# A hybrid decoder layer on one core: pinned orders, the rotary swap by transfers, four accumulators, units kept together

## The chip, the core and the metric

One core of a Trainium2 chip runs the kernel. The metric is the device time of one execution in microseconds (us), given as the median of several runs.

## What is computed

One inference step of one decoder layer, for a prompt of 1024 positions and 8 single new positions (T = 1032 columns in all), model width 1024:

```
x = x + RMSNorm(Mixer(RMSNorm(x)));  y = h + RMSNorm(SwiGLU(RMSNorm(h)))
Mixer: one input projection ->
  (a) q, k, v of 3 attention groups (window, dilation) = (128,1), (512,4), (2048,16), 8 heads x 64,
      rotary on q and k, outputs merged by their softmax denominators  -> 512
  (b) Mamba-2 scan: z / xBC / dt, 16 heads x 64, 2 groups, state 128, conv 4, chunks of 128,
      gated RMSNorm -> 1024
  concat (1536) -> one output projection -> 1024
SwiGLU: hidden 2816
def rope(x): x1, x2 = halves of 32;  [x1*cos - x2*sin, x2*cos + x1*sin]
```

Beside the two outputs y it writes the new key/value caches, the convolution rows and the scan states.

## The kernel before, in words

Data lie transposed: 128 partitions of features by T columns. Each float32 factor is split into a high and a low part of a reduced float32 format (`wh`, `wl`; `xh`, `xl`), and a product is taken as hi*hi + lo*hi + hi*lo. The work of TensorE (PE) is cut into **units** (`unit`, L168 to 176): one block of 128 output features by one of three column blocks of 344, eight 128-row slices with three products each, so 24 products into one PSUM bank. `gemm` (L189) loads a weight block (SP queue), casts it on ScalarE (ACT, L163), takes the low part on VectorE (DVE, L164), and runs three units; each unit's result is evacuated by a function that the caller gives.

PSUM has five pools: `psg` (2 banks), `pss` (2), `psa` (2), `pst` (1), `psn` (1). Main units take banks by `gps` (L180), which goes round the list `gpools`; up to the output projection this list is `[psg]`. Side work takes `pss` by `side_ps` (L80), and the attention's tiles `psa`, `pst` and `psn` by `att_ps`.

Order on each engine is set by a planner that goes by numbers of priority, the lower the sooner: `prio(kind)` (L54) hands out a rising number from a start for each kind: evac 1 million, weights 5, side 10, main 50. A PSUM slot is given in the order in which the program's text asks for it. In this frame the text runs:

- input norm, projections for the convolution and dt; the convolution on DVE
- the 16 scan steps `ssd(c, g)` (L479 to 544, eight chunks by two groups) and the decode steps `ssm_decode`, as side work. A scan step: transposes `xt` (PE), `xdt`, `xdd` (DVE), `gb` (PE), `gm` (DVE), eight subtractions `e` (DVE, L516), exp (ACT), e*gm (DVE, L519), `yp` and `yo` (PE), eb*yo (DVE), two operations on GpSimd (POOL), xg+yp and the state `hst` (DVE)
- `pattern(0)`; side `dec_scores(0)`; `pattern(1)`; side `dec_scores(1)`; `pattern(2)`; side `dec_scores(2)`, the merge of the decode outputs and the merge's weights (`wo`, `wtp`, L842). A pattern has four head pairs, each with three projections (v, q, k), the rotary step in `do_qk` and eight attention steps in `attend`. `dec_scores` (L728) transposes rows (`rtp`), sends them to DRAM, reads them back spread over partitions (`qb`), multiplies on POOL, reduces on DVE and transposes the scores (`stp`)
- the z projections (L901), the scan's gated norm, the output projection in two parts (`w_out`, then `att_part` for the attention rows)
- the FFN: for t = 0 and 1 `plain` units (gate `pg`, up `pu`, then silu), for t = 2 to 21 `blocks` that need 7 half-size products of 8, with sums of inputs (`x_sums`) taken ahead; then the output projection (`ffn_out`) and the last norm. Between, `Norms` spreads its two norm parts `first` and `second` over units counted by `GAP` and `step`.

`do_qk` (L610) makes the rotary partner `sw` by four ACT copies of 32 partitions (L615), multiplies by sin on POOL (L616) and by cos on DVE (L617), and adds (L620).

Of the kernel before, what the change touches and what calls it, by code (L numbers as in the profile page):

```python
# [25 lines left out]
LW = 388  # L26
GAP = ((1, 3), (1, 4), (2, 6))
HID = 2816
# [21 lines left out]
def trunk(tc, a, o):  # L50
    nc = tc.nc
    ctr = {"evac": 1_000_000, "w": 5_000_000, "side": 10_000_000, "late": 20_000_000, "main": 50_000_000}

# [113 lines left out]
    def unit(ps, w, hs, ls, c, ch=CH):  # L167
        wh, wl = w  # L168
        c0, c1 = ch[c]
        n = len(hs)  # L170
        with prio("main"):
            for k in range(n):
                ws = slice(k * P, (k + 1) * P)
                for j, (x, y) in enumerate(((wh, hs[k]), (wl, hs[k]), (wh, ls[k]))):
# [7 lines left out]
    def gps(name="g", cw=CW):  # L182
        q = gpools[ngp[0] % len(gpools)]
        ngp[0] += 1
        if q is psg:
            return q.tile([P, 512], F32, tag="g", name=name)[:, :cw]
        return q.tile([P, 512], F32, tag="ap", name=name)[:, :cw]

# [420 lines left out]
    def do_qk(g, hp, which):  # L609
        rw = proj_raw(g * 12 + 4 * which + hp)  # L610
        with prio("side"):
            sw = swpp.tile([P, 3 + T], F32, tag="swp", name="sw")
            for q in range(4):
                s = q ^ 1
                nc.scalar.copy(sw[q * 32:(q + 1) * 32, 0:T], rw[s * 32:(s + 1) * 32, :])  # L615
            nc.gpsimd.tensor_tensor(out=sw[:, 0:T], in0=sw[:, 0:T], in1=sin, op=ALU.mult)  # L616
            nc.vector.tensor_tensor(out=rw, in0=rw, in1=cos, op=ALU.mult)  # L617
            qp = krp if which else qrp
            qr = qp.tile([P, S], F32, tag="qr", name="qr")
            nc.vector.tensor_tensor(out=pview(qr, g), in0=porder(rw, g), in1=porder(sw, g), op=ALU.add)  # L620
            nc.vector.tensor_tensor(out=dec[which][:, g, hp], in0=rw[:, S:T], in1=sw[:, S:T], op=ALU.add)
            if which:
                if g == 1:
                    nc.sync.dma_start(out=o["pk1"][hp].rearrange("p (r i) -> p r i", r=4),
                                      in_=qr.rearrange("p (r i) -> p r i", r=4)[:, :, P:2 * P])
                else:
                    nc.sync.dma_start(out=o[f"pk{g}"][hp], in_=qr[:, S - PKW[g]:S])
        return qr

    def attend(g, hp, qr, kr, vt):  # L630
        nh = nhp.tile([P, S], F32, tag="nh", name="nh")
        for j in range(8):
# [36 lines left out]
            dst = pt[:, 0:2 * nb].rearrange("p q t -> p (q t)")  # L669
            if j % 2 and j % 4 < 2:  # L670
                nc.scalar.copy(dst, tp[:, :2 * nk])
            else:
                nc.vector.tensor_copy(dst, tp[:, :2 * nk])
            if j % 4 == 0:
# [56 lines left out]
    def dec_scores(g):  # L731
# [202 lines left out]
    gst.close()  # L934
    gpools.append(psa)
    ngp[0] = 0
# [52 lines left out]

    def stat(x, first, acc):  # L990
        if first:
            nc.scalar.activation(out=acc, in_=x, func=AF.Square)
# [12 lines left out]
    class Norms:  # L1005
# [12 lines left out]
        def first(self, prev):  # L1018
            c0, c1 = self.c0, self.c1
            with prio("evac"):  # L1020
                r = np_.tile([P, CW], F32, tag="nr", name="nr", bufs=1)
                finish(self.acc, r, prev=prev)
                self.acc = np_.tile([P, CW], F32, tag="nacc", name="nacc2")
                self.h = []
                for i in range(3):
                    n = min(3, KT - 3 * i)
                    x = np_.tile([P, 3, CW], F32, tag="xr", name="xr", bufs=3)
                    nc.sync.dma_start(out=x[:, :n], in_=a["xT"][3 * i:3 * i + n, :, c0:c1].rearrange("k p t -> p k t"))
                    self.h += [x[:, j] for j in range(n)]
                    for m in range(3 * i, 3 * i + n):  # L1030
                        mv, h = mix[m][:, c0:c1], self.h[m]
                        nc.vector.tensor_tensor(out=mv, in0=mv, in1=r, op=ALU.mult)
                        nc.vector.scalar_tensor_tensor(out=h, in0=mv, scalar=nw(MIX_POST, m), in1=h, op0=ALU.mult,  # L1033
                                                       op1=ALU.add)
                        stat(h, m == 0, self.acc)
                    nc.sync.dma_start(out=h_d[3 * i:3 * i + n, :, c0:c1].rearrange("k p t -> p k t"), in_=x[:, :n])

        def second(self, prev):
            c0, c1 = self.c0, self.c1
            with prio("evac"):  # L1040
                r = np_.tile([P, CW], F32, tag="nr", name="nr2", bufs=1)
                finish(self.acc, r, prev=prev)
                for m in range(KT):
                    mv = mix[m][:, c0:c1]
                    nc.vector.scalar_tensor_tensor(out=mv, in0=self.h[m], scalar=nw(FFN_PRE, m), in1=r, op0=ALU.mult,  # L1045
                                                   op1=ALU.mult)
                    nc.scalar.copy(fh[m][:, c0:c1], mv)
                    nc.vector.tensor_tensor(out=fl[m][:, c0:c1], in0=mv, in1=fh[m][:, c0:c1], op=ALU.subtract)  # L1048

# [8 lines left out]
    def att_part(c):  # L1058
        nm = Norms(c)
        for m in range(KT):  # L1060
# [6 lines left out]
            step(last, .5)  # L1067
        ahead.extend([(GAP[c][0], nm.first), (GAP[c][1], nm.second)])

    att_part(0)  # L1070
    att_part(1)
    for m in range(KT):
        step(gemm(a["w_out"][m][:, 512:1536], 1024, sh, sl, ssm_ev(m), cc=(2,), share=True))
    att_part(2)
    right.close()
# [17 lines left out]
    def plain(t, c, w):  # L1093
# [5 lines left out]
        with prio("evac"):  # L1099
            s = np_.tile([P, T], F32, tag="fs", name="fs", bufs=2)[:, :CW]  # L1100
            nc.scalar.activation(out=s, in_=pg, func=AF.Silu)
            next_copy(nc.vector.tensor_tensor(out=s, in0=s, in1=pu, op=ALU.mult))
# [46 lines left out]

    wslots = [(mixp, "mix")] * 8 + [(whp, "wh"), (wlp, "wl"), (whp, "wh"), (wlp, "wl")]  # L1150
    nws = [0]
# [44 lines left out]
    def blocks(t, s, w):  # L1196
# [26 lines left out]
        with prio("evac"):  # L1223
            add(u2, p1, b)
        b = prod("b22")
        with prio("evac"):
            add(v, u2, b)
        b = prod("t3")
        with prio("evac"):
            add(u3, u2, b)  # L1230
        b = prod("t4")
        with prio("evac"):
            next_copy(add(up[:, 0], u3, b))
        b = prod("t1")
        with prio("evac"):
            add(gate[:, 1], v, b)
            add(up[:, 1], u3, b)
            nc.scalar.activation(out=gate, in_=gate, func=AF.Silu)
# [22 lines left out]
    def ffn_out(gi):  # L1261
# [35 lines left out]
        accs = [acct[:, c0:c1] for c0, c1 in CL]  # L1297

        def ev(m, c, ps):
            c0, c1 = CL[c]  # L1300
# [4 lines left out]
            else:  # L1305
                sq = np_.tile([P, T], F32, tag="fs", name="fsq", bufs=2)
                nc.scalar.activation(out=sq[:, :c1 - c0], in_=fv, func=AF.Square)
                nc.vector.tensor_tensor(out=acc, in0=acc, in1=sq[:, :c1 - c0],
                                                                                 op=ALU.add)
            nc.scalar.activation(out=fv, in_=fv, func=AF.Copy, scale=nw(FFN_POST, m))  # L1310
# [8 lines left out]

        def put(c, m, r):  # L1320

            c0, c1 = CL[c]
            fv = fac[m][:, c0:c1]
            nc.vector.tensor_tensor(out=fv, in0=fv, in1=r, op=ALU.mult)
            if c < 2:
# [11 lines left out]
        for c, (c0, c1) in enumerate(CL):  # L1337
            for m in range(KT):
# [133 lines left out]
```

## Time and profile before

| | |
|---|---|
| median of 3 runs | 1892.22 us (1889.53 to 1893.98) |
| profiled execution | 1887.21 us, its span 1885.4 us |
| mean granted clock of PE | 0.975 |
| busy: PE, DVE, ACT, POOL | 1776.3 us (94%), 1151.1 (61%), 781.9 (41%), 323.0 (17%) |
| PE in time: start to 171 us | input norm, convolution and dt projections |
| 171 to 827 us | three attention patterns, the scan, the decode work |
| 827 to 1130 us | z projections, gated norm, output projection |
| 1130 to 1207 us | plain FFN units and the sums for the blocks |
| 1207 to 1603 us, then 1603 to 1885 us | FFN blocks; FFN output, last norm |

Busy time is the time in which an engine executes something; PE's overlapping products count once. The granted clock is 1 at full speed. A wait names the engine and line that waits, and the one that ended the wait.

### The profile page before, as it was taken

The numbers are of one execution on the slowest core, as the hardware profiler recorded it, in microseconds if no ns is written. First come the engines' busy times: TensorE is split into PE (matmuls) and PEld (weight loads), VectorE is DVE, ScalarE is ACT, GpSimd is POOL, SyncE is SP. The second block draws the span as 40 slices with busy tenths as digits, with TensorE's granted clock in tenths as the row PEclk, the third lists the DMA queues.
The fourth block names the chain that finished last, engine by engine and source line by source line (L and its number), as shares of the span: only waits on it lengthen the run. The fifth ranks groups of instructions, "written<-read, shape, count | busy, mean of one in ns | idle before, by whom it ended". The sixth has DMA issues, their size and how long they took to land.

```text
span 1885.4 us, 30770 instructions
## 1 busy us (share of the span) xinstructions
PE 1776.3 (94%) x12207; PEld 1658.5 (88%) x12207; DVE 1151.1 (61%) x2247; ACT 781.9 (41%) x1436; POOL 323.0 (17%) x218
## 2 busy tenths in 40 slices
PE   8999989999998899999789995999999999999995
PEld 6999877888887788988678995899999999999995
DVE  6545667677765544456676699766666665532338
ACT  5533454555554555565242345432232232531133
POOL 0000244544224311133542210000000000000020
PEclk9999999999999999999979998999999999999998
DMA  4322333443325333445755443354544445886686
GB/s 158 133 95 83 104 118 117 139 135 114 99 88 180 114 118 108 148 160 192 190 148 163 128 160 124 118 174 170 171 165 170 172 162 184 314 295 205 214 305 202
DMA packets 135056, 298.61 MB, mean 158 GB/s; under 512 B 18416, under 2 KB 85200, under 8 KB 133504
## 3 DMA queue, kind: packets, MB, share of 16 engines
q1 hardware_dynamic: 134912, 296.64, 47.6%
q8 instruction: 96, 1.57, 0.3%
q14 instruction: 48, 0.39, 0.1%
HBM read 247.49 MB, written 137.10 MB: 204 GB/s over the span
## 4 chain that ended last, share of the span: by engine, by line
PE 38%; DVE 7%; DMA 3%; issue 1%; ACT 1%; POOL 1%; SPq 0%; DVEq 0%; POOLq 0%; ACTq 0%
PE fb L1206 21%; PE g L175 15%; DMA nt<-n_d 2%; PE pg L175 1%; POOL nt L855 1%; DMA hr<-hid_d 1%; DVE xr L1033 1%; PE pu L175 1%; DVE nt L856 1%; DVE nacc L996 1%; DVE sl L925 0%; DVE wl L164 0%; DVE mix L1045 0%; DVE nt L857 0%; DVE fl L1048 0%
## 5 line engine op out<-in xcount | busy, mean ns | idle before, releaser
L175 PE MATMUL g<-xh,wh 128*128 128x344 f32 x1344 | 442.9, 330 | 9.2 <-ACT rw L586 4.9
L175 PE MATMUL g<-xl,wh 128*128 128x344 f32 x1344 | 439.8, 327 | 1.5 <-DVE xl L231 1.5
L175 PE MATMUL g<-xh,wl 128*128 128x344 f32 x1344 | 438.4, 326 | 0.5 <-DVE wl L164 0.5
L175 PEld LDWEIGHTS g<-xh,wh 128*128 128x128 f32 x1344 | 255.3, 190 | 18.9 <-ACT rw L586 7.3
L175 PEld LDWEIGHTS g<-xh,wl 128*128 128x128 f32 x1344 | 255.6, 190 | 12.3 <-issue 11.0
L175 PEld LDWEIGHTS g<-xl,wh 128*128 128x128 f32 x1344 | 255.6, 190 | 10.6 <-issue 7.7
L1206 PE MATMUL fb<-fh,wsl 128*128 128x258 f32 x1280 | 234.6, 283 | 0.9 <-DVE wsl L1176 0.8
L1206 PEld LDWEIGHTS fb<-fh,wsl 128*128 128x128 f32 x1280 | 198.0, 189 | 1.5 <-DVE wsl L1176 0.9
L1206 PE MATMUL fb<-fl,wsl 128*128 128x258 f32 x640 | 180.8, 283 | 0.0
L164 DVE TENSOR_TENSOR wl<-wr,wh 128x1024 fp32r<-128x1024 f32 (+1 forms) x93 | 114.1, 1227 | 82.6 <-ACT wh L163 82.4
L175 PE MATMUL g<-hh,wh 128*128 128x344 f32 x432 | 137.4, 320 | 0.7 <-ACT wh L163 0.7
L175 PE MATMUL g<-hh,wl 128*128 128x344 f32 x432 | 137.7, 319 | 0.2 <-DVE wl L164 0.2
L175 PE MATMUL g<-hl,wh 128*128 128x344 f32 x432 | 137.3, 320 | 0.0
L163 ACT CAST wh<-wr 128x1024 fp32r<-128x1024 f32 (+1 forms) x93 | 92.5, 995 | 106.6 <-PE g L175 97.3
L660 ACT ACTIVATE sm<-sm,ngm 128x128 f32<-128x128 f32 (+1 forms) x192 | 84.9, 443 | 107.5 <-DVE ngm L656 99.5
L1288 POOL TENSOR_TENSOR ow<-wr,ow 128x512 fp32r<-128x512 f32 x8 | 10.2, 1299 | 686.3 <-ACT ow L1287 686.3
L1206 PEld LDWEIGHTS fb<-fl,wsl 128*128 128x128 f32 x640 | 120.9, 189 | 0.0
L616 POOL TENSOR_TENSOR sw<-sw,sin 128x1032 f32<-128x1032 f32 x24 | 75.8, 3157 | 250.8 <-ACT sw L615 187.3
L615 ACT COPY sw<-rw 32x1032 f32<-32x1032 f32 x96 | 101.0, 1052 | 1.4
L1210 DVE TENSOR_TENSOR fo<-fp,fb 128x258 f32<-128x258 f32 x160 | 63.7, 419 | 57.4 <-PE fb L1206 57.2
L586 ACT COPY rw<-g 128x344 f32<-128x344 f32 x108 | 47.2, 443 | 113.2 <-PE g L175 70.6
L175 PEld LDWEIGHTS g<-hh,wh 128*128 128x128 f32 x432 | 80.9, 188 | 1.1 <-ACT wh L163 1.0
(362 smaller groups left out, 3759.7 us busy)
## 6 DMA issues: line engine op xcount, KB each, us to landing
out_skv<-in_cache SPq DMA_DIRECT2D x64, 1023.5 KB, 5.5
wr<-in_w_in SPq DMA_DIRECT2D x56, 512.0 KB, 3.7
out_skv<-in_cache SPq DMA_DIRECT2D x16, 1022.0 KB, 5.5
wr<-in_w_out SPq DMA_DIRECT2D x24, 512.0 KB, 3.6
hr<-hid_d SPq DMA_DIRECT2D x22, 516.0 KB, 5.0
hid_d<-fo SPq DMA_DIRECT2D x40, 258.0 KB, 3.1
wg<-in_w_fin SPq DMA_DIRECT2D x20, 512.0 KB, 5.5
wu<-in_w_fin SPq DMA_DIRECT2D x20, 512.0 KB, 3.6
```

The source lines that it names most:

```text
L163: nc.scalar.copy(wh[:, :cols], wr[:, :cols])
L164: nc.vector.tensor_tensor(out=wl[:, :cols], in0=wr[:, :cols], in1=wh[:, :cols], op=ALU.subtract)
L175: last = nc.tensor.matmul(ps, x[:, ws], y[:, c0:c1], start=(k == 0 and j == 0), stop=(k == n - 1 and j == 2))
L586: return nc.scalar.copy(rw[:, c0:c1], ps)
L615: nc.scalar.copy(sw[q * 32:(q + 1) * 32, 0:T], rw[s * 32:(s + 1) * 32, :])
L616: nc.gpsimd.tensor_tensor(out=sw[:, 0:T], in0=sw[:, 0:T], in1=sin, op=ALU.mult)
L660: nc.scalar.activation(out=sm[:, h, :nk], in_=sm[:, h, :nk], func=AF.Exp, scale=SCALE, bias=ngm[:, g, j, i:i + 1], accum_out=den[:, g, j, ...
L855: nc.gpsimd.tensor_tensor(out=nt, in0=nt, in1=wt, op=ALU.mult)
L856: nc.vector.tensor_tensor(out=nt[:, 0], in0=nt[:, 0], in1=nt[:, 1], op=ALU.add)
L996: nc.vector.tensor_tensor(out=acc, in0=acc, in1=sq, op=ALU.add)
L1206: nc.tensor.matmul(ps, x[:, ks], y, start=(k == 0 and j == 0), stop=(k == 3 and j == 2))
L1210: return nc.vector.tensor_tensor(out=dst, in0=x, in1=y, op=ALU.add)
```

## The change

- `unit`: the first product of each 24 keeps the kind main (50 million), the 23 others get the new kind `run` (3 million), ahead of weights, side work and main.
- `gpools` becomes `[psg, psg, pss, pss]` between pattern 0 and dec_scores(0), so that main units take `pss` banks too, and `[psg, psa]` from the output projection on.
- `do_qk`: the four copies go as transfers on SP's queue, the product with sin to DVE.
- `attend`: all copies of `pt` go to ACT (before, DVE had three of four).
- FFN: `Norms.first` is cut into `first` and `resid`; three gaps in `GAP`; the first square of `resid` and the sums `x_sums` are tied behind other instructions; t = 2 becomes plain too; the product with t1 moves from last to fourth in `blocks`; weight buffers of the blocks rotate otherwise; `hid_load` uses `rowp` for t < 2; in `ffn_out` the first operation of `put` is tied behind the last sum.

```
-GAP = ((1, 3), (1, 4), (2, 6))
+GAP = ((1, 1, 3), (1, 1, 4), (2, 4, 8))
+RUN = 24
...
-        with prio("main"):
-            for k in range(n):
...
+                with prio("main" if (3 * k + j) % RUN == 0 else "run"):
                     last = nc.tensor.matmul(ps, x[:, ws], y[:, c0:c1], start=(k == 0 and j == 0),
...
-        return q.tile([P, 512], F32, tag="ap", name=name)[:, :cw]
+        return q.tile([P, 512], F32, tag="sp" if q is pss else "ap", name=name)[:, :cw]
...
-                nc.scalar.copy(sw[q * 32:(q + 1) * 32, 0:T], rw[s * 32:(s + 1) * 32, :])
-            nc.gpsimd.tensor_tensor(out=sw[:, 0:T], in0=sw[:, 0:T], in1=sin, op=ALU.mult)
+                nc.sync.dma_start(out=sw[q * 32:(q + 1) * 32, 0:T], in_=rw[s * 32:(s + 1) * 32, :])
+            nc.vector.tensor_tensor(out=sw[:, 0:T], in0=sw[:, 0:T], in1=sin, op=ALU.mult)
...
-            if j % 2 and j % 4 < 2:
-                nc.scalar.copy(dst, tp[:, :2 * nk])
-            else:
-                nc.vector.tensor_copy(dst, tp[:, :2 * nk])
+            nc.scalar.copy(dst, tp[:, :2 * nk])
...
+    gpools[:] = [psg, psg, pss, pss]
+    ngp[0] = 0
     with prio("side"):
         dec_scores(0)
     pattern(1)
...
-    gpools.append(psa)
+    gpools[:] = [psg, psa]
...
+        def resid(self, prev):
...
-                        stat(h, m == 0, self.acc)
+                        stat(h, m == 0, self.acc, silu[-1] if silu and m == 0 else None)
...
-        ahead.extend([(GAP[c][0], nm.first), (GAP[c][1], nm.second)])
+        ahead.extend(zip(GAP[c], (nm.first, nm.resid, nm.second)))
...
-            nc.scalar.activation(out=s, in_=pg, func=AF.Silu)
+            silu.append(nc.scalar.activation(out=s, in_=pg, func=AF.Silu))
...
-    wslots = [(mixp, "mix")] * 8 + [(whp, "wh"), (wlp, "wl"), (whp, "wh"), (wlp, "wl")]
+    wslots = [(whp, "wh"), (wlp, "wl"), (whp, "wh"), (wlp, "wl")] + [(mixp, "mix")] * 8
...
+        p5 = prod("t1")
+        with prio("evac"):
+            add(v, u2, p5)
...
-            hr = np_.tile([P, T], F32, tag="xr", name="hr", bufs=3)
+            hr = (rowp.tile([P, T], F32, tag="row", name="hr") if t < 2
+                  else np_.tile([P, T], F32, tag="xr", name="hr", bufs=3))
...
-                            put(c - 1, i, r)
+                            put(c - 1, i, r, summed[0])
...
-    for t, c in ((0, 0), (0, 1), (1, 0), (1, 1)):
-        plain(t, c, pw[t])
+    for t in range(3):
+        for c in range(2):
+            plain(t, c, pw[t])
...
         x_raw(s)
-        x_sums(s)
-    for t in range(2):
+        with tc.issue_after(nm.end.ins):
+            x_sums(s)
+    for t in range(3):
         plain(t, 2, pw[t])
...
-    for t in range(2, HT):
-        w = w_blocks(t)
+    for t in range(3, HT):
+        if t == 3:
+            with tc.issue_after(nm.end.ins):
+                w = w_blocks(t)
+        else:
+            w = w_blocks(t)
```

How the instructions stand now, at three places. First, PE at the end of the scan. Before, the last scan step's pieces stand inside and between units of pattern 1 (`g` is a main unit's bank, `xt` and `stp` belong to the last scan step). Two places of it, the rows between them left out:

```order
L175 MATMUL g_5744<-xh7_119,wl_5714 128x344
L497 MATMUL xt_2760<-ident_90,xg_2754 128x128 x4
L175 MATMUL g_5744<-xl7_127,wh_5713 128x344
L175 MATMUL g_5770<-xh0_112,wh_5713 128x344
...
L175 MATMUL g_5813<-xh7_119,wl_5809 128x344
L175 MATMUL g_5813<-xl7_127,wh_5808 128x344
L539 MATMUL stp_2808<-xdd_2766,bt_2773 128x512
L175 MATMUL g_5839<-xh0_112,wh_5808 128x344
```

Between these two places lie some 60 rows, most of them main products.

In the changed kernel the whole last scan step, and behind it all of dec_scores(0) (`rtp`, `stp_4723`), stand ahead of the third unit of pattern 1's first projection, g_4788; the seven scan steps before it stand just above in the same way, without a main product between them:

```order
L499 MATMUL xt_2760<-ident_90,xg_2754 128x128 x4
L505 MATMUL gb_2769<-bg_2756 128x128
L506 MATMUL gb_2769<-ident_90,bg_2756 128x128
L525 MATMUL yp_2789<-e_2758,xdt_2765 64x128 x8
L533 MATMUL yo_2799<-bg_2756,hst_1745 128x128 x4
L541 MATMUL stp_2808<-xdd_2766,bt_2773 128x512
L738 MATMUL rtp_4654<-ident_90,dec0_404 8x128 x4
L738 MATMUL rtp_4660<-ident_90,dec1_405 8x128 x4
L738 MATMUL rtp_4666<-ident_90,dec2_406 8x128 x4
L753 MATMUL stp_4723<-ident_90,scs0_4674 32x128 x2
L754 MATMUL stp_4723<-bones_4646,prod_4650 32x2
L177 MATMUL g_4788<-xh0_112,wh_4731 128x344
```

Eight scan steps and dec_scores(0) are thus one piece without main products.

Second, PE at the end of the attention. Before, the transposes of the merge's weights, `wtp`, stand inside a z unit far behind the last attention step:

```order
L175 MATMUL g_9172<-xl6_126,wh_9115 128x344
L175 MATMUL g_9172<-xh7_119,wh_9115 128x344
L842 MATMUL wtp_8464<-ident_90,wo_8463 64x128 x3
L175 MATMUL g_9172<-xh7_119,wl_9116 128x344
L175 MATMUL g_9172<-xl7_127,wh_9115 128x344
```

Now the last attention steps (`nps_8245`), the merge of the decode outputs (`nps_8637`) and `wtp` stand one behind the other, ahead of a z unit, g_8809:

```order
L669 MATMUL ptp_8273<-ident_90,sm_8267 128x128 x2
L679 MATMUL nps_8245<-pt_8276,vt_7953 64x128 x2
L669 MATMUL ptp_8286<-ident_90,sm_8280 128x128 x2
L679 MATMUL nps_8245<-pt_8289,vt_7953 64x128 x2
L880 MATMUL nps_8637<-cvt_8638,sel_8634 8x512
L880 MATMUL nps_8637<-cvt_8650,sel_8634 8x512
L880 MATMUL nps_8637<-cvt_8662,sel_8634 8x512
L843 MATMUL wtp_8464<-ident_90,wo_8463 64x128
L177 MATMUL g_8809<-xh0_112,wh_8752 128x344
```

The z unit g_8809 now comes behind all of them.

Third, ACT on the way into the FFN. Before, casts for the blocks' sums (`xt2h`, `xt4h`) and the norm's squares stand ahead of the two silus `fs`:

```order
L1125 CAST xt2h_11236<-mix7_9534 128x258
L992 ACTIVATE nacc2_10980<-xr_10981 128x344
L995 ACTIVATE sq_10988<-xr_10981 128x344
L995 ACTIVATE sq_10993<-xr_10981 128x344
L1125 CAST xt4h_11256<-mix4_9531 128x258
...
L1125 CAST xt4h_11256<-mix7_9534 128x258
L995 ACTIVATE sq_11001<-xr_10997 128x344
...
L995 ACTIVATE sq_11024<-xr_11015 128x344
L1101 ACT_TABLE_LOAD
L1101 ACTIVATE fs_11078<-pg_11028 128x344
L1101 ACTIVATE fs_11132<-pg_11082 128x344
```

Now the silus stand ahead of squares and casts; the casts (L1137) come behind the norm's last casts `fh` (L1058):

```order
L1113 ACT_TABLE_LOAD
L1113 ACTIVATE fs_10982<-pg_10932 128x344
...
L1113 ACTIVATE fs_11042<-pg_10992 128x344
L201 ACT_TABLE_LOAD
L201 ACTIVATE nr_10987<-nps_10988,epst_94 128x344
L995 ACTIVATE nacc2_11046<-xr_11047 128x344
L1000 ACTIVATE sq_11054<-xr_11047 128x344
...
L1000 ACTIVATE sq_11090<-xr_11081 128x344
...
L1113 ACTIVATE fs_11144<-pg_11094 128x344
L1113 ACTIVATE fs_11198<-pg_11148 128x344
...
L1058 CAST fh7_10021<-mix7_9534 128x344
...
L1137 CAST xt2h_11357<-mix4_9531 128x258
```

In the changed order the first two silus come before the squares of the norm.

## Rows read from the trace of the kernel before

**Rows 1.** Stages: window length, busy (count) PE, PEld, DVE, ACT, POOL; PE clock, DMA share, GB/s
```profile
171.00:827.00 656.00, 632.30 (x4401) 552.67 (x4400) 391.73 (x960) 343.31 (x729) 206.16 (x131) 0.99 0.38 119
827.00:1130.20 303.20, 273.12 (x1601) 250.15 (x1600) 214.19 (x333) 122.36 (x204) 101.06 (x55) 0.94 0.56 167
1130.20:1207.40 77.20, 53.36 (x296) 51.01 (x294) 65.94 (x143) 38.96 (x80) 0.00 (x0) 0.85 0.31 103
1207.40:1603.00 395.60, 394.81 (x3285) 394.48 (x3286) 259.70 (x474) 112.45 (x163) 0.00 (x0) 1.00 0.50 173
```

**Rows 2.** PE's waits: line, releaser; us in total, times, longest
```profile
PE pg L175 <- ACT fs L1101: 18.3, 1, 18.3
PE sps L646 <- DVE qr L620: 10.0, 5, 4.2
```

**Rows 3.** PE's products in order of time: start us, us, engine, line
```profile
487.67 0.32 PE L175 MATMUL g<-xh,wh 128*128 128x344 f32 x1
488.77 0.32 PE L175 MATMUL g<-xh,wl 128*128 128x344 f32 x1
```

**Rows 4.** One scan step in order of time, PE and DVE
```profile
486.76 0.60 PE L497 MATMUL xt<-ident,xg 128*128 128x128 f32 x4
489.78 1.23 DVE L519 TENSOR_TENSOR e<-e,gm 128x1024 f32<-128x1024 f32 x1
494.64 1.09 PE L523 MATMUL yp<-e,xdt 128*64 128x128 f32 x16
495.66 1.16 PE L531 MATMUL yo<-bg,hst 128*128 128x128 f32 x8
499.37 0.69 DVE L536 TENSOR_TENSOR xg<-xg,yp 128x512 f32<-128x512 f32 x1
500.76 1.02 PE L539 MATMUL stp<-xdd,bt 128*128 128x512 f32 x2
```

**Rows 5.** DVE's groups, 180 to 660 us: busy us, mean ns | idle before
```profile
L516 DVE TENSOR_SCALAR e<-e,cs 128x128 f32<-128x128 f32 x128 | 36.0, 351 | 11.4 <-ACT eb L513 9.9 <-DMA e<-cs_d 1.4
```

**Rows 6.** ACT's groups, 180 to 660 us
```profile
L660 ACT ACTIVATE sm<-sm,ngm 128x256 f32<-128x256 f32 x82 | 40.9, 500 | 47.8 <-DVE ngm L656 41.5 <-PE xt L497 6.0
L660 ACT ACTIVATION_READ_ACCUMULATOR sm<-sm,ngm 128x1 f32 x116 | 21.7, 187 | 0.0
L671 ACT COPY pt<-ptp 128x512 f32<-128x512 f32 x14 | 8.0, 575 | 5.8 <-PE ptp L667 5.8
```

**Rows 7.** PE at both ends of dec_scores(0)
```profile
571.56 0.60 PE L739 MATMUL rtp<-ident,dec 128*8 128x128 f32 x4
603.84 0.59 PE L754 MATMUL stp<-ident,scs 128*32 128x128 f32 x2
```

**Rows 8.** Pattern 2's statistics on DVE, and the weights' transpose on PE
```profile
881.33 0.18 DVE L702 COPY stt<-den 128x64 f32<-128x64 f32 x1
906.83 0.57 PE L842 MATMUL wtp<-ident,wo 128*64 128x128 f32 x3 [0.51 <-DVE wo L841]
```

**Rows 9.** The page's groups of the swap, and a transfer: KB, us to landing
```profile
L615 ACT COPY sw<-rw 32x1032 f32<-32x1032 f32 x96 | 101.0, 1052 | 1.4
L616 POOL TENSOR_TENSOR sw<-sw,sin 128x1032 f32<-128x1032 f32 x24 | 75.8, 3157 | 250.8 <-ACT sw L615 187.3
y_d<-xg SPq DMA_DIRECT2D x16, 256.0 KB, 2.4
```

**Rows 10.** ACT on the way into the FFN
```profile
1161.80 0.74 ACT L1125 CAST xt2h<-mix 128x258 fp32r<-128x258 f32 x2 [11.73 <-DVE mix L1134]
1176.80 0.81 ACT L1101 ACTIVATE fs<-pg 128x344 f32<-128x344 f32 x2
```

**Rows 11.** Stretches around two drops of the clock, columns as in Rows 1
```profile
590.00:597.40 7.40, 4.04 (x24) 3.76 (x24) 4.61 (x4) 2.39 (x5) 6.12 (x4) 1.00 0.89 261
597.40:604.20 6.80, 5.83 (x23) 4.83 (x23) 5.92 (x16) 0.26 (x1) 3.32 (x2) 0.50 0.71 217
1164.00:1181.00 17.00, 3.69 (x13) 3.69 (x14) 12.46 (x31) 8.92 (x18) 0.00 (x0) 0.50 0.29 104
```

More of the change, by code (lines that the diff above doesn't have):

```diff
@@ L51, in trunk @@
     nc = tc.nc
-    ctr = {"evac": 1_000_000, "w": 5_000_000, "side": 10_000_000, "late": 20_000_000, "main": 50_000_000}
+    ctr = {"evac": 1_000_000, "run": 3_000_000, "w": 5_000_000, "side": 10_000_000, "late": 20_000_000, "main": 50_000_000}
     @contextmanager
@@ L170, in unit @@
         n = len(hs)
-        with prio("main"):
-            for k in range(n):
-                ws = slice(k * P, (k + 1) * P)
-                for j, (x, y) in enumerate(((wh, hs[k]), (wl, hs[k]), (wh, ls[k]))):
+        for k in range(n):
+            ws = slice(k * P, (k + 1) * P)
+            for j, (x, y) in enumerate(((wh, hs[k]), (wl, hs[k]), (wh, ls[k]))):
+                with prio("main" if (3 * k + j) % RUN == 0 else "run"):
                     last = nc.tensor.matmul(ps, x[:, ws], y[:, c0:c1], start=(k == 0 and j == 0),
@@ L988, in trunk, with stat @@
     fl = [actp.tile([P, T], F32R, tag="act", name=f"fl{k}") for k in range(KT)]
-    def stat(x, first, acc):
+    silu = []
+    def stat(x, first, acc, prev=None):
         if first:
-            nc.scalar.activation(out=acc, in_=x, func=AF.Square)
+            ins = nc.scalar.activation(out=acc, in_=x, func=AF.Square)
+            if prev is not None:
+                behind(ins, prev)
         else:
@@ L1022, in first @@
                 finish(self.acc, r, prev=prev)
+                self.r = r
+        def resid(self, prev):
+            c0, c1 = self.c0, self.c1
+            with prio("evac"):
+                r = self.r
                 self.acc = np_.tile([P, CW], F32, tag="nacc", name="nacc2")
@@ L1047, in second @@
                     nc.scalar.copy(fh[m][:, c0:c1], mv)
-                    nc.vector.tensor_tensor(out=fl[m][:, c0:c1], in0=mv, in1=fh[m][:, c0:c1], op=ALU.subtract)
+                    self.end = nc.vector.tensor_tensor(out=fl[m][:, c0:c1], in0=mv, in1=fh[m][:, c0:c1], op=ALU.subtract)
     ahead = []
@@ L1067, in att_part @@
             step(last, .5)
-        ahead.extend([(GAP[c][0], nm.first), (GAP[c][1], nm.second)])
+        ahead.extend(zip(GAP[c], (nm.first, nm.resid, nm.second)))
+        return nm
     att_part(0)
@@ L1073, in trunk @@
         step(gemm(a["w_out"][m][:, 512:1536], 1024, sh, sl, ssm_ev(m), cc=(2,), share=True))
-    att_part(2)
+    nm = att_part(2)
     right.close()
@@ L1224, in blocks @@
             add(u2, p1, b)
+        p5 = prod("t1")
+        with prio("evac"):
+            add(v, u2, p5)
         b = prod("b22")
         with prio("evac"):
-            add(v, u2, b)
+            add(gate[:, 1], v, b)
         b = prod("t3")
@@ L1230, in blocks @@
             add(u3, u2, b)
+            add(up[:, 1], u3, p5)
         b = prod("t4")
@@ L1233, in blocks @@
             next_copy(add(up[:, 0], u3, b))
[L1234 to L1237, printed above, removed]
             nc.scalar.activation(out=gate, in_=gate, func=AF.Silu)
@@ L1297, in ffn_out @@
         accs = [acct[:, c0:c1] for c0, c1 in CL]
+        summed = [None]
         def ev(m, c, ps):
@@ L1307, in ev @@
                 nc.scalar.activation(out=sq[:, :c1 - c0], in_=fv, func=AF.Square)
-                nc.vector.tensor_tensor(out=acc, in0=acc, in1=sq[:, :c1 - c0],
-                                                                                 op=ALU.add)
+                summed[0] = nc.vector.tensor_tensor(out=acc, in0=acc, in1=sq[:, :c1 - c0], op=ALU.add)
             nc.scalar.activation(out=fv, in_=fv, func=AF.Copy, scale=nw(FFN_POST, m))
@@ L1318, in out_unit, with put @@
             return last
-        def put(c, m, r):
+        def put(c, m, r, prev=None):
             c0, c1 = CL[c]
             fv = fac[m][:, c0:c1]
-            nc.vector.tensor_tensor(out=fv, in0=fv, in1=r, op=ALU.mult)
+            ins = nc.vector.tensor_tensor(out=fv, in0=fv, in1=r, op=ALU.mult)
+            if prev is not None:
+                behind(ins, prev)
             if c < 2:
@@ L1357, in trunk @@
     gpools.extend((pst, psn))
-    pw = [(load_w(a["w_fin"][0], 1024), load_w(a["w_fin"][HT], 1024)), (far_weights(1), far_weights(HT + 1))]
-    for t, c in ((0, 0), (0, 1), (1, 0), (1, 1)):
-        plain(t, c, pw[t])
+    pw = [(load_w(a["w_fin"][0], 1024), load_w(a["w_fin"][HT], 1024))]
+    pw += [(far_weights(t), far_weights(HT + t)) for t in (1, 2)]
+    for t in range(3):
+        for c in range(2):
+            plain(t, c, pw[t])
     assert not ahead
```

## Prediction

> **What bounds the kernel now.** I read the stages first, then the waits, then single stretches. The table of stretches by stage [rows 1] shows TensorE (PE) as the bound. In the FFN blocks (1207 to 1603 us) it works without a gap: 3285 products in 395.6 us are 0.120 us each, and nothing can be won there. What is lost lies in three other stages, as span less PE busy: attention 656.0 - 632.3 = 23.7 us; z and output projections 303.2 - 273.1 = 30.1 us; the way into the FFN 77.2 - 53.4 = 23.8 us. Clock is lost too: 0.94 granted over 303 us is some 18 us, 0.85 over 77 us some 11. Of the waits [rows 2] one is large: 18.3 us in one piece, PE behind the silu `fs`; the next, scores behind the rotary result `qr`, is 10.0 us in five.
>
> In attention a main product of 344 columns starts every 0.157 us (seven of them from 487.67 to 488.77 us [rows 3]), so a unit of 24 takes 3.8 us. All side work (the 16 scan steps of `ssd`, the `attend` steps, `dec_scores`) is strung between these units. A scan step is a chain over PE, DVE and POOL [rows 4] in which DVE's e*gm ends 4.25 us after `xt`'s start and `yp` follows 3.6 later, and costs PE only its own products, because main products fill the rest.
>
> **The change, by its effect on PE's order.** The main work's accumulators become, from pattern 1 on, two banks of `psg` and the two of `pss`. `pss` is also the pool of every side tile of `ssd`, `dec_scores` and the output weights (`xt`, `gb`, `yp`, `yo`, `stp`, `rtp`, `wtp`). Slots of a pool are given in the order of the program's text, and in the text the scan and dec_scores(0) stand ahead of pattern 1. So the third unit of pattern 1's first projection (g_4788) cannot have its bank before the whole scan is through, and PE, which takes its instructions in order, has nothing else. The built order shows it at three places; I call them R1, R2, R3.
>
> R1: ahead of g_4788 stand the last 7 to 8 steps of pattern 0's attention, a scan step, then eight scan steps back to back, then all of dec_scores(0). Before, the last eight scan steps lay each under main units. The price is the length of these chains, less what PE does for them anyway:
> - One scan step uncovered: from `xt` to the end of e*gm 486.76 to 491.01 = 4.25 us; from `yp`'s start to the end of xg+yp 494.64 to 500.06 = 5.42 us [rows 4]; the eight small subtractions, 36.0 us in 16 steps = 2.25 us a step [rows 5]. DVE's order in the changed kernel has these one behind the other, so 11.9, say 12 us. Eight: 96 us.
> - An attention step on ScalarE (ACT): two exps at 0.50, two accumulator reads at 0.19, a copy at 0.57 [rows 6] = 2.0 us; seven and a half are 15 us, the scan step ahead of them 12: 27 us.
> - dec_scores(0): from its first `rtp` to `stp` 571.56 to 603.84 = 32 us [rows 7] (store, broadcast load, eight products on POOL).
> - Less PE's own work: a scan step has 0.60 + 1.09 + 1.16 + 1.02 = 3.9 [rows 4], and two short `gb` products that are dearer than nothing and cheaper than `xt`'s 0.60 each, so 4.5; nine make 40, the rest some 10. That is in the time before already: -50.
> - R1 = 27 + 96 + 32 - 50 = **+105 us**. Lower bound: DVE's own pace for a step, five operations of 0.69, e*gm 1.23, the subtractions 2.25, `gm` like one of these 0.35 = 7.3 us, with 22 and 20 for the two other parts: 22 + 58 + 20 - 50 = +50. Upper bound: PE at half clock (below), +140. I take the chain's value, since its waits are real ones in [rows 4].
>
> R2: dec_scores(1) now stands whole ahead of a unit of pattern 2, with two units (7.5 us) as cover; 32 - 7.5, less some 8 us of attention products that stand there too: **+16 us**, between 8 and 25.
>
> R3: the last 16 attention steps of pattern 2 and the merge stand ahead of the z unit g_8809. 16 steps at up to 2.0 us are 32; from the last statistics to `wtp` took 25.5 us before (881.33 to 906.83 [rows 8]), with other work between, so I take 18; PE's own work there is 20: **+30 us**, between 15 and 50. Nothing hides it: the z units are the only main work left and queue behind it.
>
> **Other parts.**
> - Units kept together, four accumulators: PE's queue has 116 pieces of side work where it had 216. The gain is bounded below by nothing and above by the idle time. Attention: 20 of 23.7 us, as the waits there are short ones on banks and on `qr`. z and output: 20 of the 30.1 idle and the 18 of clock, since R3 takes the cover of its first part.
> - Rotary swap: 96 ACT copies of 1.05 us and 24 POOL products of 3.16 us go [rows 9]; 96 transfers of 132 KB and 24 DVE products come. For a transfer the nearest row is y_d's 256 KB, 2.4 us [rows 9]; the DVE product, of as many columns, is like e*gm, 1.23 [rows 4]. Chain 4 x 1.05 + 3.16 = 7.4 us before, about 4 now, in the 20 above. On DVE 24 x 1.23 = 30 us more in a stage where it is busy 392 of 656 [rows 1]: hidden by units; uncovered in R1 there are none. The 72 `pt` copies that go to ACT (0.57 each, 41 us) replace 101 us there: nothing. The transfers stand in SP's queue among the weight loads; those run two column blocks ahead, 6 units or 22 us. Cost between 0 and 20, I take 0 (second rival).
> - Way into the FFN: in ACT's order before, both silus stand behind the `xt` casts (the first at 1161.80 us) and the norm's squares, and come at 1176.80 [rows 10]; now they stand ahead, and the norms are in three pieces with 4 and 8 steps as gaps where there were 2 and 6. So the 18.3 us go, and the clock lost around them (0.50 from 1164 to 1181 [rows 11]). A third t done plain costs six units, 144 x 0.157 = 22.6, and saves seven half-size products of 24, 168 x 0.120 = 20.2: +2.4. Idle 23.8 + clock 11, less 2.4, less about 10 for what is late next (`nr2`, the last norm, `fh`): **-22 us**, between 0 and -32.
> - Blocks: one product moved, two buffers rotated, `hr` in another pool, the last `put` tied to a sum: PE has no gap there, 0 on either side (a wait opened would be one unit at most, 3).
>
> Sum: 105 + 16 + 30 - 20 - 20 - 22 = +89. Against the profiled execution: span 1885.4 + 89 = 1974; its own time was 1.8 above its span, so 1976; the median of the three runs is 5 above that execution: **1981 us**.
>
> **Rivals.**
> 1. Faster: the chains run at DVE's pace. Successive scan steps use two banks in turn and DVE, POOL and PE could work on neighbouring steps. With the lower bounds R1 50, R2 8, R3 15, and the gains at the idle sums 23.7 + 30.1 + 23.8 plus half the clock lost, 93: 73 - 93 = -20, **1872 us**. With all else at this end it decides at (93 - 23 + 50 - 42) / 8 = 9.8 us a scan step. For it: in DVE's new order half of the subtractions of one step sometimes come behind the next step's `xdd`. Against it: yp needs e*gm, xg+yp needs POOL's sum, which comes behind yo. Chance 0.11.
> 2. Swap transfers held in SP's queue, each waiting for its rotary input, with weight loads behind: five or six units a little late, +10 to +20: **1996**. Against it: 22 us of slack. Chance 0.10.
> 3. Half clock in R1 and R3. From 590 to 597.4 us PE was busy 4.04 of 7.4 us at clock 1.00, and the next 6.8 us were granted 0.50 [rows 11]; 0.50 is 1.2 of 2.4 GHz. In R1 PE would be busy 4.5 of 12 us. Then xt, yp and yo, 2.9 us on the chain, take twice as long: 9 x 2.9 = 26, and 10 in the other chains: **2017**. For it, the row; against it, the clock stayed at 1.00 in 590 to 597.4 itself, so a step may pass at full clock. Chance 0.22. The Trainium skill ("TensorE: Matmul & The Clock Gate", Part 1: The HAM clock gate) states that an array that has been idle is gated to half rate and freed again when busy; by that rule the trace agrees in the rows named, and this rival would be the time.
> 4. The change does not do what it says, the order is otherwise and little moves: **1890**. The order as built speaks against it. Chance 0.02.
>
> **How the numbers follow.** The forecast (chains of 10 to 13 us a step, 1945 to 2005 us) has 0.50; rivals 1 to 4 0.11, 0.10, 0.22, 0.02; 0.05 stay for worse (2040 and over). The range reaches from the forecast with low bounds for R2, R3 and the step at 10 us (-16 -8 -15, and 31 more of gain) = about 1910 to the half clock with R2 and R3 at their upper bounds, 2017 + 9 + 20 = about 2045. Outside are rival 1, 4 and half of the worst, 0.16. Faster by more than 0.2% (about what a measurement of this kernel can tell from no change): 0.12; the same 0.02; slower 0.86.
>
> **What would show it.** Right: a stretch of about 155 us between two main units, ahead of g_4788, in which PE is busy about a third, with eight `xt` 12 us apart and waits of PE on `xdt`, `e` and `scs`; a second of some 50 us before g_8809; the 18 us wait on `fs` gone; FFN blocks as before. Wrong: `xt` 8 us apart, main products between the eight scan steps, or an attention stage under 690 us. Rival 2 would show as PE waiting for `wl` or `wh` behind late `wr`, rival 3 as clock 0.5 in R1.

## The result and the profile after

The changed kernel takes **2025.88 us** (median of 4, 2025.5 to 2029.88) against 1893.1 us before (median of 4): ratio 1.070, interval 1.0663 to 1.0737. The forecast was 1981 us, slower, with a range of 1910 to 2045. The time lies in the range; sign and main mechanism were right, the size was 89 us where 138 came (span 1885.4 to 2023.7 us, the profiled executions).

The stages of the changed kernel, window, length, busy time (count) of PE, PEld, DVE, ACT, POOL, then PE's clock, DMA share, GB/s; they answer to [rows 1] one by one:

```profile
170.80:935.00 764.20, 664.94 (x4316) 575.47 (x4315) 358.53 (x876) 259.90 (x657) 128.56 (x108) 0.89 0.39 117
935.00:1293.40 358.40, 302.47 (x1689) 267.49 (x1687) 221.23 (x376) 127.69 (x254) 96.17 (x54) 0.87 0.47 146
1293.40:1369.90 76.50, 72.91 (x439) 71.43 (x438) 66.61 (x136) 39.58 (x78) 0.00 (x0) 0.96 0.43 143
1369.90:1752.90 383.00, 383.00 (x3193) 383.00 (x3193) 255.25 (x465) 110.31 (x158) 0.00 (x0) 1.00 0.52 176
```

Attention is 109 us longer, z and output 54; the way into the FFN takes as long as before but does 144 products more in it, and the blocks run as before (one t fewer). The order of PE in time, round the first of the three places of the prediction (start, length, engine, line, tiles):

```profile
417.20 0.32 PE L177 MATMUL g<-xl,wh 128*128 128x344 f32 x1
...
453.21 1.12 PE L499 MATMUL xt<-ident,xg 128*128 128x128 f32 x4 [1.94 <-DMA xg<-xs_d]
464.89 1.12 PE L499 MATMUL xt<-ident,xg 128*128 128x128 f32 x4 [0.85 <-DVE hst L544]
...
540.20 1.12 PE L499 MATMUL xt<-ident,xg 128*128 128x128 f32 x4 [0.85 <-DVE hst L544]
...
551.96 2.82 PE L738 MATMUL rtp<-ident,dec 128*8 128x128 f32 x12 [0.85 <-DVE hst L544]
...
579.40 0.59 PE L753 MATMUL stp<-ident,scs 128*32 128x128 f32 x2 [24.63 <-issue]
...
580.12 0.65 PE L177 MATMUL g<-xh,wh 128*128 128x344 f32 x1
```

From 417.20 to 580.12 us no main product runs: 163 us, 155 were forecast. The parts: attention and one scan step 36.0 us (27 forecast), eight scan steps 98.8 (96), dec_scores(0) 27.4 (32). In [rows 4] a scan step lay beside main products; here one is bare:

```profile
476.86 1.11 PE L499 MATMUL xt<-ident,xg 128*128 128x128 f32 x4 [0.27 <-DVE xg L538]
...
481.19 1.23 DVE L521 TENSOR_TENSOR e<-e,gm 128x1024 f32<-128x1024 f32 x1
...
482.52 1.98 PE L525 MATMUL yp<-e,xdt 128*64 128x128 f32 x16 [3.91 <-issue]
484.43 1.80 PE L533 MATMUL yo<-bg,hst 128*128 128x128 f32 x8
...
488.84 0.68 DVE L538 TENSOR_TENSOR xg<-xg,yp 128x512 f32<-128x512 f32 x1
488.98 0.94 PE L499 MATMUL xt<-ident,xg 128*128 128x128 f32 x4 [0.85 <-DVE hst L544]
```

From `xt` to `xt` it takes 12.1 us; `yp` begins when e*gm has ended (481.19 + 1.23). `yp` takes 1.98 us where it took 1.09, `yo` 1.80 where it took 1.16: half clock. The next view has stretches (columns as above): seven of the eight scan steps, then the two halves of the third place, R3:

```profile
453.20:540.20 87.00, 51.87 (x232) 35.69 (x232) 44.40 (x98) 15.40 (x25) 23.11 (x21) 0.56 0.29 92
...
953.40:990.00 36.60, 23.31 (x102) 13.71 (x100) 22.17 (x58) 14.51 (x48) 11.72 (x8) 0.55 0.53 169
990.00:1026.20 36.20, 21.29 (x83) 10.15 (x82) 18.68 (x71) 11.42 (x41) 6.95 (x7) 0.55 0.73 229
```

PE's waits of the changed kernel (line, releaser, us in total, times, longest):

```profile
PE yp L525 <- issue: 26.8, 8, 4.2
PE stp L753 <- issue: 24.6, 1, 24.6
PE nps L679 <- ACT pt L672: 14.8, 14, 3.7
PE sps L648 <- DVE mx L654: 12.8, 11, 1.7
PE g L177 <- ACT rw L588: 10.3, 5, 5.7
```

The large wait of [rows 2] on the silu `fs` is gone; eight waits ahead of `yp` and one of 24.6 us ahead of dec_scores' `stp` are new (`issue` stands where the profile shows no releaser), as are those of the attention steps on `pt` and `mx`.

Where the time came, by the start of one and the same main product in both traces (products counted from the first):

| main product | before, us | after, us | difference |
|---|---|---|---|
| 1728 (pattern 1 begins) | 395.4 | 393.6 | -1.8 |
| 1824 (g_4788, behind R1) | 420.9 | 580.1 | +159.3 |
| 2592 (pattern 2 begins) | 635.8 | 733.9 | +98.0 |
| 2688 (behind R2) | 663.8 | 778.3 | +114.5 |
| 3456 (z begins) | 825.9 | 935.0 | +109.1 |
| 3552 (g_8809, behind R3) | 846.7 | 1026.2 | +179.5 |
| 4032 (output projection) | 970.2 | 1137.4 | +167.2 |
| first plain FFN product | 1130.2 | 1293.4 | +163.2 |
| first block product | 1207.4 | 1369.9 | +162.5 |
| span | 1885.4 | 2023.7 | +138.3 |

Behind R1 61 us come back by product 2592, where before the scan and dec_scores stood between main products.

### The profile page after: what moved, and what is told of

The parts are those of the page before. It is cut to its first block, busy times and chain, and to the rows that moved or that the text cites. A ratio compares the mean times of both kernels' runs of the same rounds, so it can differ in the third digit from the quotient of the medians.

```text
span 2023.7 us, 30818 instructions
## 1 busy us (share of the span) xinstructions
PE 1836.7 (91%) x12183; PEld 1698.4 (84%) x12183; DVE 1115.2 (55%) x2180; ACT 699.6 (35%) x1403; POOL 240.5 (12%) x194
## 5 line engine op out<-in xcount | busy, mean ns | idle before, releaser
L1218 PE MATMUL fb<-fh,wsl 128*128 128x258 f32 x1216 | 222.3, 283 | 0.0
L1218 PEld LDWEIGHTS fb<-fh,wsl 128*128 128x128 f32 x1216 | 188.1, 189 | 0.0
L1218 PE MATMUL fb<-fl,wsl 128*128 128x258 f32 x608 | 172.1, 283 | 0.0
L165 DVE TENSOR_TENSOR wl<-wr,wh 128x1024 fp32r<-128x1024 f32 (+1 forms) x93 | 109.4, 1177 | 102.6 <-ACT wh L164 102.4
L1218 PEld LDWEIGHTS fb<-fl,wsl 128*128 128x128 f32 x608 | 115.0, 189 | 0.0
L654 DVE CUSTOM_DVE_ANT_0 sm<-sps,mask 128x128 f32<-128x128 f32 (+1 forms) x192 | 59.6, 347 | 86.9 <-PE ptp L669 59.2
L1301 POOL TENSOR_TENSOR ow<-wr,ow 128x512 fp32r<-128x512 f32 x8 | 10.2, 1295 | 658.6 <-ACT ow L1300 658.6
L177 PEld LDWEIGHTS g<-hh,wl 128*128 128x128 f32 x432 | 81.3, 188 | 0.0
```

The costliest lines, as they stand in the source:

```text
L165: nc.vector.tensor_tensor(out=wl[:, :cols], in0=wr[:, :cols], in1=wh[:, :cols], op=ALU.subtract)
L654: nc.vector.tensor_tensor_reduce(out=sm[:, h, :nk], in0=sps[h][:, c0:c0 + nk], in1=msk, scale=1.0, scalar=0.0, op0=ALU.add, op1=ALU.max, a ...
L1218: nc.tensor.matmul(ps, x[:, ks], y, start=(k == 0 and j == 0), stop=(k == 3 and j == 2))
```

## The experiments

Theory S: a main unit that shares a pool with side chains waits behind them whole. Rival U: keeping units together does it. Experiments 1 to 4 set them apart.

**1. Two banks again, the rest of the change kept.**

```
-    gpools[:] = [psg, psg, pss, pss]
-    ngp[0] = 0
```

> The changed kernel, but main units keep the two psg banks through attention and z (the switch to [psg, psg, pss, pss] left out). Theory S (shared slots: a main unit that takes a pss bank must wait, in the order of the text, behind whole side chains): the three stretches R1 (163 us without a main product, 111 net), R2 (about 16) and R3 (about 51 net) go: 2026 - 178 = 1848 us, or up to 1870 if four banks also gave the attention its gain of some 19. Rival U (the units kept together by priority hold the side work back, and PE must make up for it in one piece): the stretches stay, above 1990 us.

Measured 1913.42 us (ratio to before 1.0124, 1.0091 to 1.0156). The three stretches are gone from their places and with them 112 us, but not 178. In the trace, taken from the slowest of the four executions (1921.86 us), the attention still loses 38 us by product 3456. It loses them behind product 1728, in many gaps: 14 times two main products start more than 4 us apart, most 5 to 9, where before has 4 such places. All 14 lie at the border of a unit (the numbers of the products ahead of them, 1775, 1823, 1919, 1991 and so on, are all one short of a multiple of 24). A shorter stretch, 31.8 us without a main product, comes four units behind R3's place (product 3648); before has none there. S holds for the stretches that went; it does not explain this rest.

**2. Four banks alone, on the kernel before.** The lines taken out in 1, put into the kernel before, with the tag that `gps` needs and the later list `[psg, psa]`.

> The kernel before with the list of accumulators alone changed, [psg, psg, pss, pss] from behind pattern 0 and [psg, psa] from the output projection. Theory S: R1 is there nearly whole (eight scan steps of 12.4 us and dec_scores ahead of the same third unit, about +105), R2 +10, R3 smaller since fewer attention steps stand there (+25): about 2030 us. Rival U: no stretch without units kept together, 1885 to 1900 us.

Measured 2001.87 us (1.059, 1.0556 to 1.0624). R1 is there (136.7 us without a main product), R3 with 37.8; R2 is not to be seen (product 2688 at +85.1 after +84.7 at 2592). The whole is 28 us under the figure that I gave. U falls: no unit is kept together here.

**3. The change without units kept together.**

```
-RUN = 24
+RUN = 1
```

> The changed kernel with every product of a unit given the old priority main (RUN = 1), four banks kept. Theory S: R1 stays above 130 us, 1990 to 2030 us. Rival U: the stretches go, 1850 to 1900 us.

Measured 1986.85 us (1.0499, 1.0458 to 1.054), just below the interval of S: R1 stays (146.3 us), R3 falls from 72.8 to 37.7. So keeping units together costs 39 us here, most of it at R3: with units open this piece holds 8 attention steps and no rotary chain, in the changed kernel 16 and two.

**4. The switch to four banks moved behind pattern 1.**

```
-    gpools[:] = [psg, psg, pss, pss]
-    ngp[0] = 0
     with prio("side"):
         dec_scores(0)
     pattern(1)
+    gpools[:] = [psg, psg, pss, pss]
+    ngp[0] = 0
     with prio("side"):
         dec_scores(1)
```

> The changed kernel with the switch to [psg, psg, pss, pss] moved behind pattern 1. Theory S: R1 alone goes (163 us in one piece, 111 net), R2 and R3 stay: 2026 - 111 = 1915 us, 1905 to 1930, and a stretch of some 70 us without a main product ahead of the third z unit is still there. Rival U: R1 stays at its place, about 2020 us.

Measured 1935.24 us (1.0226, 1.0197 to 1.0254), a little above S. R1 is gone, R3 is there with 62.0 us and R2 with 16.4. What R1 gave back is 91, not 111 us, for the side work now meets kept units, as in 1.

Then, what is the rest in 1? Theory K: pieces of 24 leave side chains only the borders of units. Rival T: the swap's transfers.

**5. Two banks, units kept, the swap and the `pt` copies as before.** On 1: the lines of `do_qk` and `attend` as they stood.

> e1_two_banks with the rotary swap and the pt copies as in the kernel before (ACT copies, POOL product), units still kept together. e1 took 1913 us where the sum wanted 1848 to 1870: its attention stage loses 38 us against before in many gaps of 5 to 9 us between units. Theory K (24 products in one piece leave side work only the borders of units, so its chains lie bare there): 1905 to 1925 us. Rival T (the loss is the swap's transfers, late in SP's queue): 1865 to 1880 us.

Measured 1901.82 us (1.0038, 1.002 to 1.0055), 3 us under K's interval and 22 over T's. Without any transfer it is 33 us more than experiment 7 below: K. The new swap and copies together add 11.6 us to that. The stretch at product 3648 is still there, with 23.1 us.

**6. Two banks, units open.** On 1: `RUN = 1`.

> e1_two_banks with RUN = 1, so two banks and units open for side work, the new swap kept. Theory K: the gaps in the attention go, before's 1892 less the 24 of the FFN part, 1860 to 1875 us, faster than both kernels. Rival T: 1900 to 1915 us.

Measured 1872.71 us (0.9884, 0.9853 to 0.9916), 41 us below 1 with the same transfers: K again, and T falls as the main cause. No stretch of over 10 us is left ahead of the output projection. The attention stage, first of 1, then of 6 (columns as above), and behind them PE's wait for the evacuation `rw`, which frees a main bank, again of 1 and of 6:

```profile
170.70:863.90 693.20, 650.76 (x4345) 570.46 (x4344) 355.17 (x885) 261.67 (x667) 135.92 (x108) 0.95 0.44 129
```

```profile
170.70:836.10 665.40, 640.98 (x4399) 559.29 (x4398) 365.88 (x919) 272.46 (x698) 133.91 (x108) 0.98 0.45 136
```

```profile
PE g L177 <- ACT rw L588: 21.0, 10, 6.6
```

```profile
PE g L177 <- ACT rw L588: 3.3, 4, 1.6
```

A kept unit cannot be cut by a scores product, so ACT's and DVE's chains run on only at borders. With kept units PE idles more (42 against 24 us in the stage), and its clock is 0.95 where it is 0.98 with open ones.

**7. The FFN parts alone** (two banks, `RUN = 1`, old swap and copies).

> e6 with the old swap and pt copies: of the change only the FFN parts and the later list [psg, psa] are left. The way into the FFN gives back 24 us whatever the attention does: 1892 - 24 = 1868 us (1862 to 1875). If the swap by transfers saves time of its own, e6 is below this by the shorter chain, at most the 10 us of PE's waits on qr.

Measured 1868.67 us (0.9861, 0.9833 to 0.9889), as forecast. Between 6 and 7 the intervals overlap: with open units the swap by transfers gains nothing that can be measured.

**8. Work added to R1.** In each scan step from chunk 4 on, on the changed kernel:

```
+        if c >= 4:
+            for f in range(20):
+                nc.tensor.matmul(gb[:, 2 * P:4 * P], xh[f % 8][:, 0:P], xh[(f + 1) % 8][:, 0:2 * P], start=True, stop=True)
```

> The changed kernel with 20 products of 256 columns on data at hand added behind gb in each of the last eight scan steps (they fill a part of gb's bank that nothing reads, so only work is added, 2.3 us a step at full clock); PE waits there some 4 us for e anyway. Theory H (half clock prolongs the bare scan steps, whose xt, yp and yo are on the chain): the granted clock in R1 rises from 0.5 to near 1 and a step falls from 12.4 to 10 or 11 us, R1 145 to 155 us, although work was added. Rival (DVE and POOL alone set the step): 12.4 us or more, R1 163 us or more.

Measured, in one run: R1 159.4 us instead of 162.9, the eight steps' spacing 11.8 us instead of 12.4, total 2027.98 us, so no gain for the whole. Two stretches of 11 to 12 us inside R1, one at full clock and one near half; then, in time, yp and yo of a step at full clock:

```profile
466.00:478.00 12.00, 7.93 (x71) 6.22 (x68) 6.85 (x15) 2.47 (x4) 3.30 (x3) 1.00 0.35 100
...
500.00:511.00 11.00, 8.91 (x34) 6.83 (x33) 5.13 (x15) 2.42 (x4) 3.30 (x3) 0.54 0.36 107
```

```profile
487.64 1.09 PE L528 MATMUL yp<-e,xdt 128*64 128x128 f32 x16 [2.10 <-issue]
488.66 1.16 PE L536 MATMUL yo<-bg,hst 128*128 128x128 f32 x8
```

H holds in kind: work was added and the piece became shorter. The two steps wholly at full clock take 11.3 and 10.6 us; the same two of the changed kernel take 12.0 and 12.1, and all its spacings, at 0.50 to 0.64, are 11.7 to 13.4, 12.4 in the mean. Experiment 2 has one bare step at full clock without added work: 10.2 us, where the same step of the changed kernel, at 0.50, takes 11.7. So an estimate from these pairs is that the clock costs 1 to 1.5 us a step, not the 2.9 of rival 3. Among the steps of the changed kernel alone length does not follow the clock (at 0.50 both 11.7 and 13.4 occur), so other things move a step as much. The clock was not held throughout, and R1 missed the interval expected of H.

**9. Four banks, the second pair shared with the attention's scores.** In the list, `psa, psa` for `pss, pss`.

> The changed kernel with main units going round [psg, psg, psa, psa]: four accumulators again, but the second pair is shared with the attention's score tiles and no longer with the scan's and dec_scores' tiles. Theory S: what a main unit waits for is what the shared pool's side tiles hang on; the stretch of 163 us falls to some 35 us (8 attention steps and one scan step), R3 goes, and four or five shorter stretches of 15 to 25 us come where a whole attend stands ahead of a unit: 1890 to 1960 us in all. Rival (four banks in rotation cost this by themselves): a stretch above 100 us stays, 1990 us or more.

Measured 1981.44 us (1.0465, 1.0433 to 1.0497). The 163 us fall to 28.9, R3 to 17.0, and seven others of 15 to 32 us come, where attention steps stand ahead of a unit. So it is the sharing and what hangs on the shared pool, as S says; the sum of the many pieces was 21 us over the upper end that I gave.

**10. Three products kept together instead of 24** (on 7, `RUN = 3`).

> e7_ffn_part_alone with RUN = 3: three products of one 128-row slice kept together, 0.47 us, instead of 24, 3.8 us. Theory K (the loss comes from side chains that find no place inside a long piece): little or no loss at 3, 1865 to 1880 us. Rival (any piece kept together costs, through the priority above weights and side work): 1885 to 1905 us.

Measured **1856.93 us** (0.9806, 0.9781 to 0.983), the fastest of all and faster than 7 by intervals that barely part; its slowest execution, 1859.33, is below the fastest of 7, 1865.47. No loss, as K says, and a gain that nobody forecast. The traces do not tell where it lies. Its own is 7 us ahead of that of 7 by product 1728 (396.3 against 403.5 us), but so is that of experiment 11 (395.8), whose text is the same as 7's up to there. Of the z and output projections 262 us are left against 265. Its cause stays open.

**11 and 12. What opened the way into the FFN.** On 7: the sums' casts not tied behind the last norm; then, on that, only two plain t again.

```
-        with tc.issue_after(nm.end.ins):
-            x_sums(s)
+        x_sums(s)
```

> e7_ffn_part_alone without the tie that holds the casts of the blocks' sums behind the last norm (x_sums issued as before). ACT then casts xt2h ahead of the norm's squares again. If that order was what held the silus back, a wait of 10 to 18 us of PE comes back and the time is 1878 to 1888 us; if the plain units added as cover and the norm in three pieces did it, 1865 to 1873 us.

Measured 1866.28 us (0.9857, 0.983 to 0.9883): the tie is worth nothing.

```
-    for t in range(3):
+    for t in range(2):
```

(in both places where the plain t are run; the list of their weights, and the `blocks` loop with its tie, follow)

> e11_sums_free with two plain t as before (t = 2 back into the blocks); the silus' tie and the norm in three pieces stay. If the cover of six plain units is what hides the norm's end, a wait of PE of 10 to 20 us comes back where the last four plain units end, and the time is 1876 to 1888 us against 1866. If the silus' tie ahead of the squares is enough, there is no such wait and the time is 1860 to 1868 us, since the third plain t costs 2.4.

Measured 1881.75 us (0.9928, 0.9908 to 0.9948): 15.5 us come back. PE's wait on the last norm's sum of squares, in 12, then in 11:

```profile
PE nps L1006 <- DVE nacc L1002: 11.2, 2, 10.9
```

```profile
PE nps L1006 <- DVE nacc L1002: 5.4, 1, 5.4
```

Behind the 10.9 us stands another wait of 4.3 on the norm's casts `fh`. So cover by plain units hides most of the norm's end. The 13 us by which 12 is still below before belong to the rest (silus ahead of the squares, the norm in three pieces, the product with t1 and the other ties); they were not taken apart.

Put one behind the other, medians: before 1892 to 1895; FFN parts 1868.7 (-26); swap and copies 1872.7 (+4, within the uncertainty); units of 24 kept 1913.4 (+41); four banks with side pools 2025.9 (+112).

## Why the prediction came out as it did

- **Bound and stages.** Right outside the three places: PE stays the bound and the blocks are gapless; the offset to before stays at 143.8 to 143.9 us from product 5328 to 8000.
- **R1, +105.** 163 us against 155, shown by 1, 2, 4 and 9 to come from the shared slots. The step of 12 us was right partly by luck, for two things that cancel: at full clock it is 10.2 to 11.3 us (experiments 2 and 8), as DVE's subtractions begin beside `xt` (482.44 where `xt` begins at 481.98, experiment 8) and I counted them behind one another, and the clock was half. The piece ahead of the eight was 9 us longer.
- **R2, +16.** +16.5 us from product 2592 to 2688.
- **R3, +30.** This term failed in size: 72.8 us without a main product where I had 50. I counted 16 attention steps, and left out the rotary chains of the last heads, which lie in this piece too and end at 971.3 us, 18 us behind its start. DVE's rows there:

```profile
954.25 1.23 DVE L618 TENSOR_TENSOR sw<-sw,sin 128x1032 f32<-128x1032 f32 x1 [13.71 <-DMA sw<-rw]
955.40 1.23 DVE L619 TENSOR_TENSOR rw<-rw,cos 128x1032 f32<-128x1032 f32 x1
957.39 1.97 DVE L622 TENSOR_TENSOR qr<-rw,sw 128x1024 f32<-128x1024 f32 x1
...
964.81 1.23 DVE L618 TENSOR_TENSOR sw<-sw,sin 128x1032 f32<-128x1032 f32 x1 [3.10 <-DMA sw<-rw]
```

  The first waited 13.71 us for its transfers, nearly all of it ahead of R3's start at 953.4; so the chains slid into R3. All of `rw` had been evacuated by 934 us, but SP issued them only at 949.93:

```profile
933.50 0.45 ACT L588 COPY rw<-g 128x344 f32<-128x344 f32 x1 [1.97 <-PE g L177]
...
945.36 0.33 SPq L689 DMA_DIRECT2D n_d<-nh  x1
949.30 0.60 PE L606 MATMUL vtp<-ident,vp 128*128 128x128 f32 x4
949.93 2.45 SPq L617 DMA_DIRECT2D sw<-rw  x4
...
959.22 0.22 DVE L623 TENSOR_TENSOR dec<-rw,sw 128x8 f32<-128x8 f32 x1
959.46 2.41 SPq L617 DMA_DIRECT2D sw<-rw  x4
```

  The store `n_d` ahead of them in SP's queue was issued at 945.36 and does not explain the last 4 us. What ended last are the transposes `vtp` (949.30 + 0.60): they read `vp`, which comes from the same pool `swpp` of two buffers as `sw` (L600, L614). The second `sw`'s transfers came in the same way right behind `dec`, the last reader of the first `sw`. So what ended the wait was a buffer coming free, not rival 2's queue, and no term of mine had it. Both come with kept units: experiment 3, with open ones, has neither the rotary chains nor the first 8 of the 16 steps in this piece, and there it takes 37.7 us. Half clock (0.55 in both halves of R3) adds to it; how much was not taken apart.
- **"Units kept together, four accumulators": -20 and -20.** The step of the prediction that failed outright. I wrote that the gain is bounded below by nothing, because PE's queue has fewer switches. No row said so. Experiments 1 against 6, 5 against 7 and the change against 3 price the piece of 24 at +41, +33 and +39 us. Between product 3456 and the first FFN product the sum had +10 and the trace +54; experiment 3's trace, with open units, has +27, so the kept units make most of what I missed, R3's longer piece among it. In the attention it shows little beside the four banks: +109 measured, +101 forecast, +99 in experiment 3.
- **Way into the FFN, -22.** -22.3 us by the last block product (163.2 to 140.9); the FFN output and the last norm, which I had at 0, give another 2.6 (to 138.3). Alone, in 7, all of it is -26. I named ACT's order and the gaps and booked the third plain t as a cost of 2.4 us; experiment 12 shows it as a gain of 15.5, against 13 for all the rest.
- **Swap, 0.** The transfers land after 2.4 us, as y_d's did ([rows 9]):

```profile
sw<-rw SPq DMA_DIRECT2D x96, 129.0 KB, 2.4
```

  With open units it gains nothing measurable; with kept units it and the copies cost 11.6 us together; which of the two was not tried.
- **Rivals.** 1 would have needed steps under 9.8 us; none came below 10.2 in experiments 2, 3 and 8. 3 was right on the clock (0.56 over seven of the eight steps) and two to three times too dear. By the rule of the Trainium skill ("TensorE: Matmul & The Clock Gate", Part 1: The HAM clock gate) an idle array is gated and a busy one freed; the trace agrees in direction, in that PE, busy 51.87 of 87.00 us, stayed near half and had longer stretches at 1.00 with added work (466.00 to 478.00 us in experiment 8). 4 fell with the order.

## What to carry to other kernels

Ahead of sharing a pool between main units and side chains, read in the built order what stands between two main units, and price that piece bare: here eight chains that took PE only for their own products beside other work cost 99 us alone. A piece of work kept together on the bound engine must be short against the side chains' steps: 3 products did no harm and 24 cost 33 to 41 us. A buffer of a shared pool in SBUF can hold a chain just as a bank in PSUM does: look at what ended last before you blame a queue. Never set one end of a term to zero because a count went down; ask what the longer piece keeps waiting.

## What the runs showed of the hardware

Adding work made a stretch shorter: with 20 more products a step, R1 fell from 162.9 to 159.4 us (one trace of each); some steps then ran at clock 1.00, with yp at 1.09 us where it took 1.98. In the same piece a stretch with PE busy 8.91 of 11.00 us was granted 0.54, and one with 7.93 of 12.00 us 1.00. At half clock the same products take longer, so busy share alone does not tell the clock.
